# Mixed channels stored as a high and a low part, and a sample tile that carries both in one operand

## The chip, the cores and the metric

One core of a Trainium2 chip runs one program. Its engines are TensorE (PE, matrix products, and PEld for loading its stationary operand), VectorE (DVE), ScalarE (ACT), GpSimd (POOL) and SyncE (SP, which issues most transfers). Each engine takes its instructions in the order in which they stand. The metric is the device time of one execution in microseconds; lower is better.

## What is computed

One inference step of a layer for 1024 prompt tokens and 64 sample tokens, 1024 channels wide. A normalised input is projected once; its columns feed two head groups, and both are gated, joined to 2048 mixed channels and projected back:

```python
proj = h @ w_in
...
o = _diff_attend(q, k, v, ...)                    # group A: differential attention, 8 heads
y_a = o.reshape(bsz, t_len, A_WIDTH) * jax.nn.silu(proj[..., A_G:B_R].astype(F32))
...
yb, s_T = _wkv_scan(rh, hs(decay), kh, vh, -kk, kk * ah, wkv0.astype(F32))   # group B: RWKV-7
yb = (yb + bonus.reshape(bsz, t_len, B_WIDTH)) * jax.nn.silu(proj[..., B_G:IN_TOTAL].astype(F32))
mix = jnp.concatenate([y_a, yb], axis=-1).astype(x.dtype)
out = mix @ w_out
x_new = x + _rms_norm(out, norm_post, NORM_EPS)
```

## The kernel before

Products of float32 values are made from two parts: a high part (a cast to fp32r) and a low part (the rest). `split` (L155) makes them: ScalarE copies the value to the high part, GpSimd subtracts that from the value. A product of two such values is three matrix products: high by high, low by high, high by low.

The program is written by streams (Python generators) that `Weave` (L59) interleaves as it is built. A stream yields either a modelled time after which it may go on or a condition; the stream of lowest rank that can go on is taken next. `spend` adds to the modelled time of TensorE, `op` books an operation on another engine and returns when it should be done. So the order on each engine is fixed when the program is built, and a change of these numbers changes it.

Head group B comes first (`phase_b`, L290): 17 units, of channel pair p and half hf of the prompt, and one of all pairs for the sample. A unit ends with its gated result `yo` (L941 to L964), channels by 512 tokens, which SyncE stores to the DRAM tile `mixd["B", hf]` (L969). The input projections are the filler between the units. Then comes attention (`phase_a`, L1238): per head h and query tile qt the streams `score` and `qtile`; after the last query tile of a group of four (or the sample's), the gated result `y` (L1485) goes to `mixd["A", j]` (L1487).

The filler of that stage is the output projection (`out_projection`, L1096). It works through 63 jobs (g, tt): 7 groups of four channel blocks (groups 0 to 5 with one half of the output columns, the last with both) by 9 token tiles, 8 of 128 prompt tokens and the sample's, number 8. `load_wo` loads and splits the weights of a group. `load_mix` (L1148) loads the job's 4 x 128 channels by 128 tokens to `raw` (two buffers, tag mxr; for the sample, zeros fill the 64 empty columns, L1157) and splits them to `hi` and `lo` (three buffers each, tags mxh and mxl). The loader starts a job's load when the job three back has been issued. A job is 12 products of 128 x 512 per column half:

```python
mm(ps, hi[:, q, :], wh, start=(q == 0), stop=False)
mm(ps, lo[:, q, :], wh, start=False, stop=False)
mm(ps, hi[:, q, :], wl, start=False, stop=(q == len(ks) - 1))
```

Their sum is added to `part[tt]` (L1225, L1228). In the last group `half_done` (L1180) squares each half on ScalarE, and `finish` (L1189) normalises the row, adds x and stores it; for tiles 3 and 8 a quarter of the columns goes to ScalarE and GpSimd. PSUM has two buffers for these sums (`pjp`).

Of the kernel before, what the change touches and what calls it, by code (L numbers as in the profile page):

```python
# [11 lines left out]
F32 = mybir.dt.float32  # L12
# [9 lines left out]
P = 128  # L22
# [95 lines left out]
def layer(ctx: ExitStack, tc: tile.TileContext, I, O):  # L118
# [76 lines left out]
    mixd = {(a, j): tc.dram_tile([D, n], F32, name=f"mix{a}{j}")  # L195
# [94 lines left out]
def phase_b(tc, I, O, E):  # L290
# [8 lines left out]
    with ExitStack() as bs:  # L299
# [203 lines left out]
        def unit(n, p, hf):  # L503
# [437 lines left out]
            yo = t512("ysq", 1, nm=f"o{u}")  # L941
            for g in range(2):
# [23 lines left out]
            if smp:  # L966
                nc.sync.dma_start(out=mixd["B", 2].rearrange("(q c) t -> c q t", c=P), in_=c3(yo))
            else:
                nc.sync.dma_start(out=mixd["B", hf][p * P:(p + 1) * P, :], in_=yo)  # L969
# [126 lines left out]
def out_projection(tc, I, O, E):  # L1096
# [24 lines left out]
    jobs = [(g, tt) for g in range(7) for tt in ((4, 5, 6, 7, 0, 1, 2, 3, 8) if g == LAST else range(9))]  # L1121
# [26 lines left out]
    def load_mix(q):  # L1148
# [6 lines left out]
        raw = op.tile([P, 4, P], F32, tag="mxr", bufs=2, name=f"mxr{g}{tt}")[:, 0:m]  # L1155
        if n < P:
            nc.gpsimd.memset(raw, 0.0)  # L1157
        r0 = (ks[0] % 8) * P
        nc.sync.dma_start(out=raw[:, :, 0:n], in_=src[r0:r0 + m * P, o_ * P:o_ * P + n].rearrange(
            "(k c) t -> c k t", c=P))  # L1160
        yield W_DMA
        hi = op.tile([P, 4, P], F32R, tag="mxh", bufs=MB, name=f"mxh{g}{tt}")[:, 0:m]
        lo = op.tile([P, 4, P], F32R, tag="mxl", bufs=MB, name=f"mxl{g}{tt}")[:, 0:m]
        yield split_op(hi, lo, raw, m * P)
        mix[q] = hi, lo
# [14 lines left out]
    def half_done(tt, ch):  # L1180

        if ch == 0:
            x_ = op.tile([P, D], F32, tag="x", bufs=2, name=f"fx{tt}")
            nc.scalar.dma_start(out=x_[:P if tt < 8 else TS], in_=x_rows(tt))
            fin[tt] = x_, op.tile([P, 2], F32, tag="ms", bufs=2, name=f"fm{tt}")
        sq = op.tile([P, 512], BF16, tag="sq", name=f"fs{tt}{ch}")
        act(sq, part[tt][:, ch * 512:(ch + 1) * 512], AF.Square, accum_out=fin[tt][1][:, ch:ch + 1])

    def finish(tt):  # L1189
# [3 lines left out]

        vts(ms[:, 0:1], ms[:, 0:1], ms[:, 1:2], D * NORM_EPS, op0=ADD, op1=ADD)
        gtt(ms[:, 0:1], ms[:, 0:1], nh[:, 0:1], op=POW)
        m = 768 if tt in (3, 8) else D
        a, b = o_[:, 0:m], o_[:, m:]
        if m < D:
            act(b, b, AF.Copy, scale=ms[:, 0:1])
        stt(a, a, ms[:, 0:1], npb[:, 0:m], op0=MUL, op1=MUL)  # L1200
        vtt(a[:n], a[:n], x_[:n, 0:m], op=ADD)
        if m < D:
            gtt(b, b, npb[:, m:], op=MUL)
            gtt(b[:n], b[:n], x_[:n, m:], op=ADD)
# [353 lines left out]
```

## Time and profile before

| | us |
|---|---|
| median of 3 runs | 1828.87 (1828.2 to 1833.91) |
| profiled execution | 1827.69 |
| its span | 1825.9 |
| PE busy in the span | 1685.0 (92%) |
| DVE | 1248.1 (68%) |
| ACT | 846.3 (46%) |
| POOL | 721.5 (40%) |

A busy share is a mean over stages. Group B fills the time to about 1260 us, attention the time to about 1740, the rest of the output projection the time to 1815. Matrix products are pipelined: one may start before the row of the one before has ended, so the distance of starts, not the duration of a row, tells what one of them takes of TensorE. A wait is put down to what came last before the instruction could start.

### The profile page before, as it was taken

The numbers are of one execution on the slowest core, as the hardware profiler recorded it, in microseconds if no ns is written. First come the engines' busy times: TensorE is split into PE (matmuls) and PEld (weight loads), VectorE is DVE, ScalarE is ACT, GpSimd is POOL, SyncE is SP. The second block draws the span as 40 slices with busy tenths as digits, with TensorE's granted clock in tenths as the row PEclk, the third lists the DMA queues.
The fourth block names the chain that finished last, engine by engine and source line by source line (L and its number), as shares of the span: only waits on it lengthen the run. The fifth ranks groups of instructions, "written<-read, shape, count | busy, mean of one in ns | idle before, by whom it ended". The sixth has DMA issues, their size and how long they took to land.

```text
span 1825.9 us, 34303 instructions
## 1 busy us (share of the span) xinstructions
PE 1685.0 (92%) x12930; PEld 1505.6 (82%) x12930; DVE 1248.1 (68%) x2600; ACT 846.3 (46%) x2026; POOL 721.5 (40%) x905
## 2 busy tenths in 40 slices
PE   5999989999998989999999989989998899988997
PEld 4988978889878888898898878989887777777885
DVE  5577777786777877778778567654466566677736
ACT  5334443444434444444444333333455665766632
POOL 3432332332332232333333333111443758667563
PEclk9999999999999999999999989999999899999999
DMA  5110123121132111121111121336745555644345
GB/s 154 53 56 26 51 64 91 33 65 49 44 85 64 33 52 33 30 67 30 42 46 31 59 70 46 106 105 152 183 121 151 162 157 162 165 123 123 96 137 165
DMA packets 204096, 158.82 MB, mean 87 GB/s; under 512 B 44085, under 2 KB 185050, under 8 KB 203930
## 3 DMA queue, kind: packets, MB, share of 16 engines
q1 hardware_dynamic: 169098, 137.33, 26.4%
q10 hardware_dynamic: 34832, 19.30, 4.1%
q8 instruction: 102, 1.67, 0.4%
q14 instruction: 64, 0.52, 0.1%
HBM read 108.67 MB, written 47.34 MB: 85 GB/s over the span
## 4 chain that ended last, share of the span: by engine, by line
PE 56%; DVE 19%; POOL 7%; DMA 6%; issue 5%; ACT 4%; ACTq 1%; SPq 1%; POOLq 0%; DVEq 0%
PE x_o L1456 2%; PE po L1217 2%; PE po L1218 2%; PE po L1219 2%; PE cbank L871 2%; PE cbank L843 2%; PE m_s L670 1%; PE pj_av L215 1%; PE s L1395 1%; PE cbank L860 1%; PE pj_av L216 1%; PE pj_av L217 1%; PE pj_g L215 1%; PE s L1396 1%; PE pj_aq L215 1%
## 5 line engine op out<-in xcount | busy, mean ns | idle before, releaser
L850 ACT ACTIVATE sd<-suv,dc 64x64 f32<-64x64 f32 x128 | 44.4, 347 | 178.3 <-DVE suv L881 151.1
L1217 PE MATMUL po<-woh,mxh 128*128 128x512 f32 x288 | 121.6, 422 | 1.5 <-DVE part L1228 0.9
L1219 PE MATMUL po<-wol,mxh 128*128 128x512 f32 x288 | 115.1, 400 | 1.8 <-POOL wol L158 1.8
L1218 PE MATMUL po<-woh,mxl 128*128 128x512 f32 x288 | 115.4, 401 | 0.9 <-POOL mxl L158 0.9
L1412 ACT ACTIVATE e<-s,nb 128x128 f32<-128x128 f32 (+7 forms) x144 | 101.1, 707 | 31.9 <-DVE nb L1405 20.8
L158 POOL TENSOR_TENSOR mxl<-mxr,mxh 128x512 fp32r<-128x512 f32 x63 | 88.2, 1401 | 54.9 <-ACT mxh L157 52.5
L1456 PE MATMUL x_o<-vn,wt 128*128 128x128 f32 (+1 forms) x608 | 87.1, 289 | 11.4 <-DVE wt L1446 3.7
L1456 PEld LDWEIGHTS x_o<-vn,wt 128*128 128x128 f32 (+1 forms) x608 | 80.0, 200 | 20.6 <-DVE wt L1446 5.2
L1405 DVE TENSOR_REDUCE nb<-s 128x1 f32<-128x640 f32 (+8 forms) x104 | 95.5, 921 | 2.0
L716 POOL TENSOR_TENSOR ltlo<-lt,lt 64x512 f16<-64x512 f32 x32 | 37.6, 1176 | 130.3 <-ACT lt L704 129.1
L1395 PE MATMUL s<-k,qs 128*128 128x512 f32 (+4 forms) x208 | 75.8, 372 | 7.8 <-ACT e L1412 6.0
L881 DVE SCALAR_TENSOR_TENSOR suv<-cbank,dc,sd 64x64 f32<-64x64 f32 x224 | 63.1, 282 | 29.2 <-PE cbank L871 24.2
L871 PE MATMUL cbank<-suv,bkt 128*128 128x128 f32 x256 | 56.4, 302 | 23.1 <-DVE suv L867 23.1
L215 PE MATMUL pj_k<-hhi,wh_k 128*128 128x384 f32 (+1 forms) x192 | 72.1, 375 | 3.8 <-ACT raw_k L230 3.8
L1396 PE MATMUL s<-k,qs 128*128 128x512 f32 (+4 forms) x208 | 70.6, 357 | 2.8 <-POOL k L1325 1.8
L215 PE MATMUL pj_av<-hhi,wh_av 128*128 128x384 f32 (+1 forms) x192 | 69.8, 363 | 2.3 <-DVE fl_g L980 2.1
L215 PE MATMUL pj_aq<-hhi,wh_aq 128*128 128x384 f32 (+1 forms) x192 | 70.8, 369 | 0.0
L215 PE MATMUL pj_g<-hhi,wh_g 128*128 128x384 f32 (+1 forms) x192 | 70.6, 368 | 0.0
L215 PE MATMUL pj_ak<-hhi,wh_ak 128*128 128x384 f32 (+1 forms) x192 | 70.2, 366 | 0.0
L871 PEld LDWEIGHTS cbank<-suv,bkt 128*128 128x128 f32 x256 | 41.3, 189 | 34.4 <-DVE suv L867 32.1
L215 PE MATMUL pj_v<-hhi,wh_v 128*128 128x384 f32 (+1 forms) x192 | 69.6, 363 | 0.0
L1228 DVE TENSOR_TENSOR part<-po,part 128x512 f32<-128x512 f32 x54 | 37.0, 686 | 47.0 <-PE po L1219 46.8
(525 smaller groups left out, 6044.1 us busy)
## 6 DMA issues: line engine op xcount, KB each, us to landing
mxr<-mixB SPq DMA_DIRECT2D x32, 256.0 KB
wor<-in_w_out SPq DMA_DIRECT2D x64, 128.0 KB
qa<-scr_q SPq DMA_DIRECT2D x32, 204.0 KB
ka<-scr_k SPq DMA_DIRECT2D x32, 204.0 KB
mxr<-mixA SPq DMA_DIRECT2D x24, 256.0 KB
scr_q<-fl_q SPq DMA_DIRECT2D x8, 544.0 KB
scr_k<-fl_k SPq DMA_DIRECT2D x8, 544.0 KB
scr_v<-fl_v SPq DMA_DIRECT2D x8, 544.0 KB
```

Of the source, the lines that this page charges most:

```text
L158: gtt(lo, raw, hi.bitcast(F32), op=SUB)
L215: mm(ps[:, :n], hi[:, k, :], hhi[i][:, k, :], start=(k == 0), stop=False)
L871: mm(s, bkt[:, c], suv[:, c], start=True, stop=True)
L881: stt(suv[r, c + 1, h, :] if c < 7 and not smp else to[r], s[r, h * CH:(h + 1) * CH], dc[r, c:c + 1], sd[r], op0=MUL, op1=ADD)
L1217: mm(ps, hi[:, q, :], wh, start=(q == 0), stop=False)
L1218: mm(ps, lo[:, q, :], wh, start=False, stop=False)
L1219: mm(ps, hi[:, q, :], wl, start=False, stop=(q == len(ks) - 1))
L1395: mm(s2[:, b:b + w], lq, k1[c][:, k0 + o_:k0 + o_ + w], start=True, stop=False)
L1396: mm(s2[:, b:b + w], lq, k2[c][:, k0 + o_:k0 + o_ + w], start=False, stop=True)
L1405: nc.vector.tensor_reduce(nb[:, 0:m], s3[:, :, 0:n], axis=AX.X, op=MAX, negate=True)
L1412: act(e[:, 0:n], s3[:, j, 0:n], AF.Exp, bias=nb[:, j:j + 1], accum_out=st["sm"][:, c:c + 1])
L1456: mm(ops[:, 0:P], wt[0:w, b, :], vn[0:w, vb, :], start=(b == 0), stop=(b == len(kbs) - 1))
```

## The change

Both parts of a mixed channel are made where it is made: at the end of a unit of group B (`yo` becomes the low part in place, `yh` the high part) and at the end of a group of query tiles in attention. Both are stored, in pieces of 128 tokens; the DRAM tile has the high and the low part of a token tile side by side. `load_mix` then loads both in one transfer of 512 KB (256 KB for the sample) straight into the products' operand `mx`, three buffers, with no split behind it and no zeros. For the sample, `mx` has 64 columns of high and 64 of low parts, so that one product yields high by weight in rows 0 to 63 and low by weight in rows 64 to 127: two products per block where there were three (low by low is added too). At the end the lower rows of `part[8]` are moved up by a transfer and added. In the last group the sample stands between tiles 7 and 0 and no longer at the end, and in attention its last head's sample tile between query tiles 4 and 3.

```diff
-    mixd = {(a, j): tc.dram_tile([D, n], F32, name=f"mix{a}{j}")
+    mixd = {(a, j): tc.dram_tile([D, n // min(n, P), 2, min(n, P)], F32, name=f"mix{a}{j}")
...
             yo = t512("ysq", 1, nm=f"o{u}")
+            yh = t512("yh", 1, F32R, nm=f"h{u}")
...
             op_(DVE, 512)
-            if smp:
-                nc.sync.dma_start(out=mixd["B", 2].rearrange("(q c) t -> c q t", c=P), in_=c3(yo))
-            else:
-                nc.sync.dma_start(out=mixd["B", hf][p * P:(p + 1) * P, :], in_=yo)
+            w = TS if smp else P
+            yl = yo.bitcast(F32R)
+            split(yh, yl, yo)
+            op_(ACT, 512)
+            yield op_(POOL, 512)
+            for s, t in ((0, yh), (1, yl)):
+                t_ = t.bitcast(F32).rearrange("p (c t) -> p c t", t=w)
+                if smp:
+                    nc.sync.dma_start(out=mixd["B", 2][:, 0, s].rearrange("(q c) t -> c q t", c=P), in_=t_)
+                else:
+                    nc.sync.dma_start(out=mixd["B", hf][p * P:(p + 1) * P, :, s], in_=t_)
             free.add(("g", p, hf))
...
-    jobs = [(g, tt) for g in range(7) for tt in ((4, 5, 6, 7, 0, 1, 2, 3, 8) if g == LAST else range(9))]
+    jobs = [(g, tt) for g in range(7) for tt in ((4, 5, 6, 7, 8, 0, 1, 2, 3) if g == LAST else range(9))]
...
-        raw = op.tile([P, 4, P], F32, tag="mxr", bufs=2, name=f"mxr{g}{tt}")[:, 0:m]
-        if n < P:
-            nc.gpsimd.memset(raw, 0.0)
         r0 = (ks[0] % 8) * P
-        nc.sync.dma_start(out=raw[:, :, 0:n], in_=src[r0:r0 + m * P, o_ * P:o_ * P + n].rearrange(
-            "(k c) t -> c k t", c=P))
+        mx = op.tile([P, 4, 2 * P], F32, tag="mx", bufs=MB, name=f"mx{g}{tt}")[:, 0:m, 0:2 * n]
+        nc.sync.dma_start(out=mx, in_=src[r0:r0 + m * P, o_].rearrange("(k c) s t -> c k (s t)", c=P))
         yield W_DMA
-        hi = op.tile([P, 4, P], F32R, tag="mxh", bufs=MB, name=f"mxh{g}{tt}")[:, 0:m]
-        lo = op.tile([P, 4, P], F32R, tag="mxl", bufs=MB, name=f"mxl{g}{tt}")[:, 0:m]
-        yield split_op(hi, lo, raw, m * P)
-        mix[q] = hi, lo
+        mix[q] = mx.bitcast(F32R)
...
     def half_done(tt, ch):
 
+        if tt == 8:
+
+            if ch == 0:
+                return
+            low = op.tile([P, D], F32, tag="x", bufs=2, name="low")[0:TS]
+            nc.sync.dma_start(out=low, in_=part[8][TS:P])
+            vtt(part[8][0:TS], part[8][0:TS], low, op=ADD)
+            half(tt, 0)
+        half(tt, ch)
...
-        m = 768 if tt in (3, 8) else D
+        m = 768 if tt in (2, 3) else D
...
-                mm(ps, hi[:, q, :], wh, start=(q == 0), stop=False)
-                mm(ps, lo[:, q, :], wh, start=False, stop=False)
-                mm(ps, hi[:, q, :], wl, start=False, stop=(q == len(ks) - 1))
-                spend(690)
+                end = q == len(ks) - 1
+                if tt == 8:
+
+                    mm(ps, mx[:, q, :], wh, start=(q == 0), stop=False)
+                    mm(ps, mx[:, q, :], wl, start=False, stop=end)
+                    spend(460)
+                else:
+                    mm(ps, mx[:, q, 0:P], wh, start=(q == 0), stop=False)
+                    mm(ps, mx[:, q, P:], wh, start=False, stop=False)
+                    mm(ps, mx[:, q, 0:P], wl, start=False, stop=end)
+                    spend(690)
...
-            xdone(op_(DVE, n_))
-            nc.sync.dma_start(out=mixd["A", j][h * P:(h + 1) * P, :], in_=y[:, 0:n_])
+            yield xdone(op_(DVE, n_))
+            yh = ap_.tile([P, HALF], F32R, tag="yh", name=f"yh{u}")
+            w = n_ // m
+            split(yh[:, 0:n_], y[:, 0:n_].bitcast(F32R), y[:, 0:n_])
+            op_(ACT, n_)
+            yield op_(POOL, n_)
+            for s, t in ((0, yh.bitcast(F32)), (1, y)):
+                nc.sync.dma_start(out=mixd["A", j][h * P:(h + 1) * P, :, s],
+                                  in_=t[:, 0:n_].rearrange("p (c t) -> p c t", t=w))
             yield 3000
...
-        for o_, qt in enumerate((0, 1, 8, 2, 3, 4, 5, 6, 7) if h < 7 else (7, 6, 5, 4, 3, 2, 1, 0, 8)):
+        for o_, qt in enumerate((0, 1, 8, 2, 3, 4, 5, 6, 7) if h < 7 else (7, 6, 5, 4, 8, 3, 2, 1, 0)):
```

GpSimd in group B, where the first unit (pair 0, first half) ends; `bk` belongs to the unit that follows it, `t_wus` is the split of a later unit's small weights, `wl_aq3` the low part of a projection weight. Before:

```order
L917 COPY ycp_517<-ycp_517 64x64
L634 TENSOR_TENSOR bk1_0_2371<-t_kb1_0_2026,t_cs1_0_1918 64x8x64
L425 MEMSET mv1_1_2447 128x64
L426 MEMSET mv1_1_2447 128x64
L533 TENSOR_TENSOR t_wus1_10_2609<-t_wup1_2477,t_wus1_10_2609 128x256
L158 TENSOR_TENSOR wl_aq3_2425<-wr_aq30_2426,wh_aq3_2424 128x512
L379 COPY sh_495<-raw_v1_2174 128x1
L380 COPY sh_495<-raw_v1_2174 128x1
```

Now:

```order
L918 COPY ycp_517<-ycp_517 64x64
L635 TENSOR_TENSOR bk1_0_2373<-t_kb1_0_2026,t_cs1_0_1918 64x8x64
L426 MEMSET mv1_1_2451 128x64
L427 MEMSET mv1_1_2451 128x64
L158 TENSOR_TENSOR ysq_o0_0_2298<-ysq_o0_0_2298,yh_h0_0_2299 128x512
L534 TENSOR_TENSOR t_wus1_10_2613<-t_wup1_2481,t_wus1_10_2613 128x256
L158 TENSOR_TENSOR wl_aq3_2429<-wr_aq30_2430,wh_aq3_2428 128x512
L380 COPY sh_495<-raw_v1_2174 128x1
```

The subtraction of `ysq_o0_0` by `yh_h0_0` stands ahead of the next unit's weight split.

SyncE where the output projection begins; `mxr00` and `mx00` are the first job's tile, `wor` pieces of w_out, `ka` the k rows of a later head. Before:

```order
L1357 DMA out_k_s<-kt82_17299 64x128
L1159 DMA mxr00_17230<-mixB0_123 128x4x128
L1141 DMA wor800_17234<-in_w_out 128x256
L1159 DMA mxr01_17236<-mixB0_123 128x4x128
L1301 DMA ga2_16804<-scr_g2_152 128x1088
L1141 DMA wor80256_17312<-in_w_out 128x256
L1360 DMA out_v_p<-vn2_16802 128x8x128
L1159 DMA mxr02_17291<-mixB0_123 128x4x128
L1361 DMA out_v_s<-vn2_16802 64x128
L1487 DMA mixA1_121<-y1_7_17349 128x512
L1141 DMA wor900_17354<-in_w_out 128x256
L1276 DMA ka30_17391<-rot_k02_166 16x1088
```

Now:

```order
L1380 DMA out_k_s<-kt82_17412 64x128
L1166 DMA mx00_17321<-mixB0_123 128x4x256
L1150 DMA wor800_17325<-in_w_out 128x256
L1166 DMA mx01_17327<-mixB0_123 128x4x256
L1166 DMA mx02_17331<-mixB0_123 128x4x256
L1150 DMA wor80256_17368<-in_w_out 128x256
L1150 DMA wor900_17397<-in_w_out 128x256
L1150 DMA wor90256_17407<-in_w_out 128x256
L1150 DMA wor1000_17430<-in_w_out 128x256
L1383 DMA out_v_p<-vn2_16878 128x8x128
L1384 DMA out_v_s<-vn2_16878 64x128
L1396 DMA out_k_p<-kt20_17439 128x8x64
```

Three tiles and five weight pieces stand ahead of the first `ka` transfer (it comes three rows later), where three tiles and three pieces stood.

VectorE in the last group: `po6` and then tile and column half are the sums, `fm` the statistics, `fx` the rows of x. Before, at the end:

```order
L1228 TENSOR_TENSOR part3_17221<-po631_21941,part3_17221 128x512
L1228 TENSOR_TENSOR part8_17226<-po680_21965,part8_17226 128x512
L1194 TENSOR_SCALAR fm3_21938<-fm3_21938 128x1
L1200 SCALAR_TENSOR_TENSOR part3_17221<-part3_17221,fm3_21938,npb_17227 128x768
L1201 TENSOR_TENSOR part3_17221<-part3_17221,fx3_21936 128x768
L1228 TENSOR_TENSOR part8_17226<-po681_21984,part8_17226 128x512
L1194 TENSOR_SCALAR fm8_21981<-fm8_21981 128x1
L1200 SCALAR_TENSOR_TENSOR part8_17226<-part8_17226,fm8_21981,npb_17227 128x768
L1201 TENSOR_TENSOR part8_17226<-part8_17226,fx8_21979 64x768
```

Now, where the sample is finished:

```order
L1251 TENSOR_TENSOR part8_17317<-po681_21689,part8_17317 128x512
L1251 TENSOR_TENSOR part0_17309<-po600_21716,part0_17309 128x512
L1251 TENSOR_TENSOR part0_17309<-po601_21735,part0_17309 128x512
L1191 TENSOR_TENSOR part8_17317<-part8_17317,low_21699 64x1024
L1251 TENSOR_TENSOR part1_17310<-po610_21758,part1_17310 128x512
L1210 TENSOR_SCALAR fm8_21704<-fm8_21704 64x1
L1216 SCALAR_TENSOR_TENSOR part8_17317<-part8_17317,fm8_21704,npb_17318 64x1024
L1210 TENSOR_SCALAR fm0_21732<-fm0_21732 128x1
L1217 TENSOR_TENSOR part8_17317<-part8_17317,fx8_21702 64x1024
L1216 SCALAR_TENSOR_TENSOR part0_17309<-part0_17309,fm0_21732,npb_17318 128x1024
L1251 TENSOR_TENSOR part1_17310<-po611_21777,part1_17310 128x512
L1217 TENSOR_TENSOR part0_17309<-part0_17309,fx0_21730 128x1024
```

The addition of `low` stands behind both sums of tile 0, and the sample's steps between those of tiles 0 and 1.

## Rows read from the trace of the kernel before

**Rows 1.** The head and PE's part of the page's first part

```profile
span 1825.9 us, 34303 instructions
PE 1685.0 (92%) x12930; PEld 1505.6 (82%) x12930; DVE 1248.1 (68%) x2600; ACT 846.3 (46%) x2026; POOL 721.5 (40%) x905
```

**Rows 2.** By stretch, us: length; PE, PEld, DVE, ACT, POOL busy; clock; DMA share

```profile
100.00:1300.00 1200.00, 1129.82 (x9766) 1032.70 (x9765) 860.77 (x1905) 493.75 (x1119) 369.25 (x434) 0.99 0.22 62
1400.00:1740.00 340.00, 308.11 (x1784) 255.72 (x1784) 225.63 (x431) 216.15 (x591) 224.25 (x286) 0.96 0.52 143
1740.00:1764.00 24.00, 23.67 (x104) 19.05 (x103) 5.84 (x9) 8.77 (x20) 20.80 (x24) 1.00 0.50 148
1764.00:1815.00 51.00, 50.15 (x220) 40.77 (x218) 33.00 (x41) 17.46 (x43) 16.36 (x18) 1.00 0.53 173
1815.00:1826.00 11.00, 0.25 (x2) 0.00 (x0) 4.68 (x6) 1.23 (x3) 4.91 (x5) 0.62 0.23 72
```

**Rows 3.** Timeline of PE; columns: start us, us, engine, line, operation

```profile
1740.32 0.39 PE L1218 MATMUL po<-woh,mxl 128*128 128x512 f32 x1
1740.55 0.39 PE L1219 MATMUL po<-wol,mxh 128*128 128x512 f32 x1
1740.77 0.39 PE L1217 MATMUL po<-woh,mxh 128*128 128x512 f32 x1
```

**Rows 4.** Instructions of the mix tile; ns are least, median, most

```profile
L157 ACT CAST mxh<-mxr x63: 603/620/667, 1413.6 to 1799.0; 128x512 fp32r<-128x512 f32 x63
L158 POOL TENSOR_TENSOR mxl<-mxr,mxh x63: 1263/1290/2447, 1414.3 to 1799.7; 128x512 fp32r<-128x512 f32 x63
L1157 POOL MEMSET mxr<- x7: 525/527/529, 1463.9 to 1790.4; 128x512 f32 x7
```

**Rows 5.** The gated result of attention (same view)

```profile
L1485 DVE SCALAR_TENSOR_TENSOR y<-x_z,dv,ga x24: 274/743/752, 1320.6 to 1736.2; 128x512 f32<-128x512 f32 x16, 128x64 f32<-128x64 f32 x8
```

**Rows 6.** Waits of PE from 1300 us; columns: total us, times, longest

```profile
PE s L1395 <- ACT e L1412: 6.0, 6, 2.5
```

**Rows 7.** Timeline of POOL and DVE in the last group

```profile
1784.65 1.29 POOL L158 TENSOR_TENSOR mxl<-mxr,mxh 128x512 fp32r<-128x512 f32 x1
1784.72 2.30 DVE L1200 SCALAR_TENSOR_TENSOR part<-part,fm,npb 128x1024 f32<-128x1024 f32 x1 [0.73 <-POOL fm L1195]
...
1792.29 1.28 DVE L1200 SCALAR_TENSOR_TENSOR part<-part,fm,npb 128x1024 f32<-128x1024 f32 x1 [0.67 <-POOL fm L1195]
```

**Rows 8.** Waits of SyncE's queue from 1300 us

```profile
SPq L1159 <- POOL mxl L158: 77.1, 35, 5.8
```

**Rows 9.** Issue and cast of a load (timeline); the chain's longest load

```profile
1758.68 3.10 SPq L1159 DMA_DIRECT2D mxr<-mixA  x2
1761.47 0.62 ACT L157 CAST mxh<-mxr 128x512 fp32r<-128x512 f32 x1 [1.45 <-DMA mxr<-mixA]
...
1409.24 6.83 DMA mxr<-mixB
```

**Rows 10.** Group B: a unit's last step, a weight split, a PE wait

```profile
L964 DVE TENSOR_TENSOR ysq_o<-ysq_o,mg x16: 680/687/693, 207.6 to 1261.8; 128x512 f32<-128x512 f32 x16
...
L158 POOL TENSOR_TENSOR wl_v<-wr_v,wh_v x16: 1266/1376/1836, 67.8 to 964.7; 128x512 fp32r<-128x512 f32 x16
...
PE cbank L871 <- DVE suv L867: 23.1, 23, 3.2
```

**Rows 11.** Instructions of the result rows on DVE

```profile
L1228 DVE TENSOR_TENSOR part<-po,part x54: 664/691/692, 1497.8 to 1816.5; 128x512 f32<-128x512 f32 x54
L1200 DVE SCALAR_TENSOR_TENSOR part<-part,fm,npb x9: 1017/1285/2301, 1772.9 to 1818.9; 128x1024 f32<-128x1024 f32 x7, 128x768 f32<-128x768 f32 x2
L1201 DVE TENSOR_TENSOR part<-part,fx x9: 1207/1225/1366, 1774.7 to 1819.9; 128x1024 f32<-128x1024 f32 x7, 128x768 f32<-128x768 f32 x1, 64x768 f32<-64x768 f32 x1
```

**Rows 12.** The last product (timeline); the queue's wait for the last store

```profile
1814.86 0.39 PE L1219 MATMUL po<-wol,mxh 128*128 128x512 f32 x1
...
SPq L1554 <- DMA out_xs<-part: 2.4, 1, 2.4
```

More of the change, by code (lines that the diff above doesn't have):

```diff
@@ L1180, in half_done, with half @@
     def half_done(tt, ch):
+        if tt == 8:
[6 more added lines that the diff above has]
+        half(tt, ch)
+    def half(tt, ch):
+        n = P if tt < 8 else TS
         if ch == 0:
             x_ = op.tile([P, D], F32, tag="x", bufs=2, name=f"fx{tt}")
-            nc.scalar.dma_start(out=x_[:P if tt < 8 else TS], in_=x_rows(tt))
+            nc.scalar.dma_start(out=x_[:n], in_=x_rows(tt))
             fin[tt] = x_, op.tile([P, 2], F32, tag="ms", bufs=2, name=f"fm{tt}")
         sq = op.tile([P, 512], BF16, tag="sq", name=f"fs{tt}{ch}")
-        act(sq, part[tt][:, ch * 512:(ch + 1) * 512], AF.Square, accum_out=fin[tt][1][:, ch:ch + 1])
+        act(sq[:n], part[tt][:n, ch * 512:(ch + 1) * 512], AF.Square, accum_out=fin[tt][1][:n, ch:ch + 1])
     def finish(tt):
@@ L1192, in finish @@
         x_, ms = fin.pop(tt)
+        ms = ms[:n]
         vts(ms[:, 0:1], ms[:, 0:1], ms[:, 1:2], D * NORM_EPS, op0=ADD, op1=ADD)
-        gtt(ms[:, 0:1], ms[:, 0:1], nh[:, 0:1], op=POW)
-        m = 768 if tt in (3, 8) else D
-        a, b = o_[:, 0:m], o_[:, m:]
+        gtt(ms[:, 0:1], ms[:, 0:1], nh[:n, 0:1], op=POW)
+        m = 768 if tt in (2, 3) else D
+        a, b = o_[:n, 0:m], o_[:n, m:]
         if m < D:
             act(b, b, AF.Copy, scale=ms[:, 0:1])
-        stt(a, a, ms[:, 0:1], npb[:, 0:m], op0=MUL, op1=MUL)
-        vtt(a[:n], a[:n], x_[:n, 0:m], op=ADD)
+        stt(a, a, ms[:, 0:1], npb[:n, 0:m], op0=MUL, op1=MUL)
+        vtt(a, a, x_[:n, 0:m], op=ADD)
         if m < D:
-            gtt(b, b, npb[:, m:], op=MUL)
-            gtt(b[:n], b[:n], x_[:n, m:], op=ADD)
+            gtt(b, b, npb[:n, m:], op=MUL)
+            gtt(b, b, x_[:n, m:], op=ADD)
         dst = O["xp"][0, tt * P:(tt + 1) * P, :] if tt < 8 else O["xs"][0]
@@ L1210, in out_projection @@
         yield lambda: g in ws and i in mix
-        hi, lo = mix.pop(i)
+        mx = mix.pop(i)
         ks, chs = groups[g]
@@ L1241, in phase_a @@
     nh, ident, hsl = (E[k] for k in ("nh", "ident", "hsl"))
-    scr, mixd, mixed, weave = (E[k] for k in ("scr", "mixd", "mixed", "weave"))
+    scr, mixd, mixed, weave, split = (E[k] for k in ("scr", "mixd", "mixed", "weave", "split"))
     projected, roped = E["projected"], E["roped"]
```

## Prediction

> **What bounds the kernel now.** I read the page's busy shares first, then the busy time by stage, then single starts on TensorE, then the waits. TensorE is busy for 1685.0 of 1825.9 us [rows 1]; no other engine is above 68%. By stages [rows 2] the reader is to see three different pictures. From 100 to 1300 us (head group B with projections woven in) TensorE is busy 1129.82 of 1200 us, so 70.2 us are idle. From 1400 to 1740 (attention with the output projection woven in) it is busy 308.11 of 340, 31.9 us idle. From 1740 to 1815 only the output projection is left: 23.67 of 24 and 50.15 of 51. There TensorE alone is the bound, and its products start 0.227 us apart (1740.32, 1740.55, 1740.77) though a row says 0.39, because they are pipelined [rows 3]. So in that stretch a product that goes is worth 0.227 us, not the 0.40 of a mean duration. The end is an in-order TensorE queue: its work plus its idle time, plus the last 11 us, in which it is busy for 0.25 [rows 2].
>
> **Products that go.** Each product in L1217 to L1219 is one of three per channel block and column half. The sample has 16 blocks and 2 halves, so with pairs in place of triples 32 of its 96 products go. 32 x 0.227 = 7.3 us. Sixteen of them (groups 4, 5 and the last) belong to the stretch in which nothing else runs before, 3.6 us; the other sixteen stand among attention work, where idle time could take their place. I take -7.3, bounds -3.6 and -7.3, since in an in-order queue the work behind them moves up.
>
> **Splits that go, in the attention stage.** Before, each of 63 jobs has a cast of 0.62 on ScalarE and a subtraction of 1.29 (median) on GpSimd, 7 also a memset of 0.53 [rows 4]: 39.1, over 81 and 3.7 us. 24 new splits come back, after each y; 16 are 512 columns wide [rows 5], at the same prices 10 and 21 us, 8 have 64 columns and cost less. GpSimd loses some 60 of the 224.25 us that it is busy from 1400 to 1740, ScalarE some 27 of 216.15 [rows 2]. Neither is the bound, so this is not a gain by itself; it is one only where TensorE waits for them or for VectorE. Such waits are there, each short: the longest in sum are scores waiting for the exponential on ScalarE, 6.0 us in 6 waits [rows 6]. VectorE gains too: at 1784.72 a product-and-scale took 2.30 us while GpSimd's subtraction (1784.65, 1.29 us) ran, the same step at 1792.29 beside no such work took 1.28, so 1.02 us of collision [rows 7]. The Trainium skill (SBUF — State Buffer, section "Who interferes with whom") says that a VectorE instruction with two SBUF inputs contends with a GpSimd instruction that reads SBUF, and the second blocks for the whole of the first; that would make it about 1.22 + 1.28 = 2.50 here, and the row's 2.30 is near it. Idle time of 31.9 us cannot shrink by more than half, since most of it waits for TensorE's own results to come round; bounds 0 and -16, and I take -4, nearer the waits that rows name than the whole.
>
> **A wait that is added.** The load of a tile now writes straight into the operand (3 buffers), so it waits on SyncE for the products of the job three back; before, it waited for GpSimd's subtraction, 77.1 us in 35 waits [rows 8]. Queued behind it on SyncE are the next head's q and k loads, weights and stores, as before. In the pure stretch two jobs lie between, 24 products or 5.45 us; while attention runs it is longer. A 256 KB load took 2.8 us (issued 1758.68, cast released at 1761.47) when little else moved and 6.83 at 1409.24 in a crowd [rows 9]. The new load is twice the bytes in as many pieces, and no row shows it. At 2.8 it costs nothing; at 6.83 it misses by 1.4 us per job, for the five or so narrow jobs left in that stretch: +7. In the last group the two jobs take 10.9 us and cover either. I take 0, bounds 0 and +7. SyncE's order at the start of the output projection now has three loads and five weight pieces ahead of the next head's k loads, where three loads and three pieces stood; the share of the transfer engines from 1400 to 1740 is 0.52 [rows 2], so there is room, and I count nothing.
>
> **Splits that come, in group B.** 17 units get a cast, a subtraction and a second store behind their last VectorE step. The step before them takes 0.69, and a subtraction of this size among projections 1.38 [rows 10]. No later step of the same unit waits for them; what is queued behind them on GpSimd is the next unit's weight split, as the order shows. With the cast and a collision on VectorE, a unit costs 0.62 + 1.38 + 1.02 = 3.0 us at most if all of it lands on TensorE's path, 51 in all; nothing if it falls into idle time (GpSimd is busy 369.25 of 1200 us). TensorE's largest named wait there is for VectorE's copies in the state chain, 23.1 us in 23 waits [rows 10], so a VectorE that is held up can reach TensorE. I take +3, near the lower end, bounds 0 and +51. The changed waits also reorder some projections; that has no sign.
>
> **The end of the last group.** The sample moves before tiles 0 to 3, and its low half comes by a transfer and an addition on VectorE. The order puts both adds of tile 0 ahead of that addition, so a transfer of 2.8 us is hidden by 5.45 us of products. VectorE's load is then two adds of 0.69, 1.28 and 1.23 per tile [rows 11], 3.9 of 5.45 us, and the sample's 1.2 more in one place: TensorE can be held for a buffer once, I reckon 1 us, and the collisions above that go were worth up to 0.85 us of idle. Net 0, bounds -0.9 and +3. The last store is of 128 rows, not 64: the queue waits 2.4 us for 256 KB now [rows 12], bounds 0 and +2.4, I take +0.5. The tail from the last product (1814.86, [rows 12]) keeps its steps.
>
> **Sum.** -7.3 - 4 + 0 + 3 + 0 + 0.5 = -7.8 us. The profiled execution has a span of 1825.9 in 1827.69 us, so 1819.9 for its like. The median of the runs is 1828.87, 1.2 above the profiled one; **1821**.
>
> **Rivals.** (a) The attention stage tightens to its bound, -16 in place of -4: 1809. For it: GpSimd stands between statistics and transposes all through that stage, and the collisions on VectorE go. Against it: TensorE names few waits for GpSimd. (b) The products go but idle time takes their place outside the pure stretch: -3.6, relief 0, +3, +0.5, so 1829, no change. For it: 31.9 us idle in short waits for results that are no faster. Against it: the filling work is never short there. (c) Slower: the new splits in group B sit ahead of the next unit's weight split on GpSimd and hold VectorE. Half of their full price, 26 in place of 3, gives +15: 1844. It decides from about 1 us per unit (16.3 us in all, against the 10.8 of the other terms, for 5.5 more than before). For it: VectorE's state chain is what TensorE waits for. Against it: the splits lie off every chain. If VectorE alone is held, 17 collisions of 1.02 us [rows 7] that all reach TensorE add 17 in place of 3: 1835, at the edge of slower. The Trainium skill's rule above is what would make VectorE block wherever the two overlap. That the sample keeps its triples is no rival: the change writes pairs.
>
> **How the numbers follow.** Forecast 0.55 (its own range 1813 to 1827), (a) 0.13, (b) 0.20, (c) 0.12, of which 0.04 for the collisions alone. A difference under 0.3%, 5.5 us, can hardly be told from none. Below 1823.4 lie (a) and 0.45 of the forecast: faster 0.58. Between lie 0.10 of the forecast and (b): same 0.30. Slower 0.12. The range reaches from (a) to past (b), 1808 to 1833, and leaves out (c) and little else.
>
> **What would show it.** Right: 32 products fewer in the output projection; TensorE's idle time in the attention stage some 4 us below 31.9; group B's end within a few us of where it was; no wait of TensorE for the tile's load above 1 us in all. Wrong: TensorE waiting for the load (the wait of three jobs), VectorE's busy time in group B up by more than 10 us (c), an idle stretch at the sample's addition, or an idle time between the two that has moved by more than the saving.

## Result: slower by 2.9%, lost in two places

The changed kernel takes 1884.16 us (median of 4 runs, 1878.64 to 1890.19) against 1828.53 us of the kernel before: a ratio of 1.029, 95% interval 1.027 to 1.032. The forecast was 1821 us, a gain; the range 1808 to 1833 did not hold the time. The profiled execution took 1885.55 us. Its page begins, as [rows 1] did for the kernel before:

```profile
span 1883.8 us, 34243 instructions
...
PE 1709.2 (91%) x12898; PEld 1521.4 (81%) x12898; DVE 1245.9 (66%) x2601; ACT 833.6 (44%) x2004; POOL 675.8 (36%) x876
```

GpSimd has lost 45.7 us of work and ScalarE 12.7, as foreseen, and the span is longer by 58. So the work that went was not on the path. The question is by stage: I cut both executions at the same events, the last transposes of group B's last unit (1256.6 before, 1284.0 after), the first tile load of the output projection (1408, 1437.5), the last store of attention's results (1736.5, 1816) and the last product. Busy times by stretch: columns are length, then PE, PEld, DVE, ACT, POOL busy, then the granted clock, the share of the transfer engines and GB/s. The kernel before:

```profile
100.00:1256.60 1156.60, 1090.46 (x9548) 995.78 (x9546) 843.00 (x1868) 476.81 (x1082) 358.21 (x425) 0.99 0.20 57
1256.60:1408.00 151.40, 141.26 (x894) 129.53 (x892) 85.52 (x175) 81.53 (x213) 58.22 (x78) 0.97 0.59 150
1408.00:1736.50 328.50, 298.38 (x1728) 247.59 (x1727) 221.18 (x418) 209.47 (x568) 217.73 (x279) 0.96 0.52 144
1736.50:1815.00 78.50, 77.32 (x338) 62.73 (x336) 39.94 (x52) 28.43 (x68) 39.52 (x44) 1.00 0.51 162
```

and the changed kernel:

```profile
100.00:1284.00 1184.00, 1100.09 (x9543) 1005.41 (x9541) 850.35 (x1870) 486.78 (x1101) 376.01 (x443) 0.98 0.21 59
1284.00:1437.50 153.50, 144.76 (x916) 133.73 (x914) 89.11 (x177) 84.03 (x219) 65.52 (x85) 0.96 0.58 154
1437.50:1816.00 378.50, 330.43 (x1781) 266.17 (x1780) 215.93 (x423) 199.85 (x556) 181.96 (x263) 0.91 0.62 176
1816.00:1875.00 59.00, 56.04 (x244) 45.18 (x242) 35.45 (x47) 12.82 (x35) 7.67 (x10) 1.00 0.68 216
```

Group B is 27.4 us longer with the same products. The output projection, from its first load to its last product, is 29.9 us longer (437.1 against 407.2) with 32 products fewer: attention's part has grown by 50 us, and more of the projection was done in it, so the rest is 19.5 shorter. In attention's part TensorE idles 48.1 us where it idled 30.1, and the granted clock is 0.91 where it was 0.96. If TensorE were never idle, that would be (1 - 0.91) x 378.5 = 34 us against 13, an estimate from above.

### The profile page after: what moved, and what is told of

Same layout as the page of the kernel before. It is cut to its first block, busy times and chain, and to the rows that moved or that the text cites. A ratio compares the mean times of both kernels' runs of the same rounds, so it can differ in the third digit from the quotient of the medians.

```text
span 1883.8 us, 34243 instructions
## 1 busy us (share of the span) xinstructions
PE 1709.2 (91%) x12898; PEld 1521.4 (81%) x12898; DVE 1245.9 (66%) x2601; ACT 833.6 (44%) x2004; POOL 675.8 (36%) x876
## 3 DMA queue, kind: packets, MB, share of 16 engines
q1 hardware_dynamic: 200554, 162.10, 29.9%
## 4 chain that ended last, share of the span: by engine, by line
PE 42%; DVE 16%; POOL 6%; issue 4%; ACT 3%; DMA 3%; ACTq 0%; POOLq 0%; SPq 0%; DVEq 0%
PE x_o L1479 3%; PE po L1242 2%; PE po L1240 2%; PE po L1241 2%; PE s L1418 2%; PE s L1419 2%; PE pj_ag L216 1%; PE x_wt L1465 1%; PE cbank L872 1%; PE pj_ag L217 1%; PE pj_ag L218 1%; PE m_s L671 1%; POOL wol L158 1%; DVE xt L738 1%; PE cbank L861 1%
## 5 line engine op out<-in xcount | busy, mean ns | idle before, releaser
L1435 ACT ACTIVATE e<-s,nb 128x256 f32<-128x256 f32 (+8 forms) x144 | 100.7, 706 | 51.9 <-DVE nb L1428 37.0
L1240 PE MATMUL po<-woh,mx 128*128 128x512 f32 x256 | 111.9, 437 | 6.1 <-ACT woh L157 3.0
L1242 PE MATMUL po<-wol,mx 128*128 128x512 f32 x256 | 105.9, 415 | 11.6 <-POOL wol L158 11.5
L1241 PE MATMUL po<-woh,mx 128*128 128x512 f32 x256 | 105.4, 412 | 0.0
L872 PE MATMUL cbank<-suv,bkt 128*128 128x128 f32 x256 | 56.8, 304 | 20.9 <-DVE suv L868 20.9
L1469 DVE COPY wt<-x_wt 128x512 f32<-128x512 f32 (+3 forms) x64 | 37.1, 586 | 57.3 <-PE x_wt L1465 57.0
L1242 PEld LDWEIGHTS po<-wol,mx 128*128 128x128 f32 x256 | 50.3, 197 | 27.1 <-POOL wol L158 16.9
```

What stands on the lines that cost most here:

```text
L872: mm(s, bkt[:, c], suv[:, c], start=True, stop=True)
L1240: mm(ps, mx[:, q, 0:P], wh, start=(q == 0), stop=False)
L1241: mm(ps, mx[:, q, P:], wh, start=False, stop=False)
L1242: mm(ps, mx[:, q, 0:P], wl, start=False, stop=end)
L1435: act(e[:, 0:n], s3[:, j, 0:n], AF.Exp, bias=nb[:, j:j + 1], accum_out=st["sm"][:, c:c + 1])
```

## Experiments on group B: the plan or the work

The theories: the split's own work slows the units, or the bookings and the pause behind it have moved the projections in the plan. Four kernels tell them apart. The first two start from the changed kernel.

```diff
 # b_nobook
             split(yh, yl, yo)
-            op_(ACT, 512)
-            yield op_(POOL, 512)
 # b_nosplit
-            split(yh, yl, yo)
...
-            for s, t in ((0, yh), (1, yl)):
+            for s, t in ((0, yl), (1, yl)):
```

> The changed kernel, but the plan no longer counts the group-B split: its two bookings and the pause behind it are left out, the split and its two stores are still issued. TensorE's order up to the last unit of group B is then that of the kernel before, row for row; with the bookings 1608 of its 11256 rows stand elsewhere. The last unit's transposes of the changed kernel end 27 us later than before (1284 against 1257). Theory order (the moved projections cost it): they end within 6 us of 1257 and the kernel takes about 1857. Theory split work (cast, subtraction and the second store cost it, 1.3 us in each of units 2 and 3, which stand before any row is moved): they end at 1279 to 1284 and the kernel takes 1879 to 1884.

> The changed kernel with the plan's bookings kept, but group B's cast and subtraction left out: the whole value is stored into both slots (so the B part of the result counts the value twice). TensorE's order is that of the changed kernel; stores, bytes and loads are the same. Theory order: nothing comes back, the last unit's transposes end at about 1284 and the kernel takes about 1884. Theory split work: they end at 1257 to 1263 and the kernel takes about 1860.

b_nobook: 1860.06 us, the last unit's transposes at 1266. b_nosplit: 1869.15 us, 1275. Both theories hold in part: of group B's 27 us some 18 are order and some 9 are work (1266.2 - 1256.6 = 9.6 with the old order and the splits; 1284.0 - 1275.3 = 8.7 when the splits go). The order's part was then put on the kernel before by itself:

```diff
 # before_book
             op_(DVE, 512)
+            op_(ACT, 512)
+            yield op_(POOL, 512)
```

> The kernel before, with the two bookings and the pause that the change has behind group B's last step, and nothing else: no instruction is added or left out, the plan alone reckons with a split that does not exist. Earlier runs put 18 of the 27 us that group B got longer down to the moved projections (the changed kernel without the bookings ended its last unit's transposes at 1266, with them at 1284). Theory order: here they end at 1272 to 1278 in place of 1257, and the kernel takes 1842 to 1852. Theory that the order costs only beside real splits: 1257 to 1262, and 1829 to 1835.

1850.20 us, ratio 1.012 (1.009 to 1.016), the transposes at 1277.7: 21 us for two numbers and a pause, with no work added on any engine. TensorE's waits in group B (to 1290 us in the changed kernel, to 1256 in the others) are its signature. Columns: who waited for whom, us in total, times, longest. Before, b_nobook, before_book, changed kernel:

```profile
PE m_ip L723 <- DVE x L742: 7.3, 8, 2.5
...
PE cbank L860 <- DVE gsb L857: 4.6, 8, 1.8
```

```profile
PE m_ip L724 <- DVE x L743: 7.3, 8, 2.5
...
PE cbank L861 <- DVE gsb L858: 6.7, 9, 1.8
```

```profile
PE m_ip L723 <- DVE x L742: 18.7, 14, 2.7
...
PE cbank L860 <- DVE gsb L857: 14.0, 15, 2.3
```

```profile
PE m_ip L724 <- DVE x L743: 18.7, 14, 2.7
...
PE cbank L861 <- DVE gsb L858: 15.9, 17, 2.3
```

The pairs go with the order, not with the splits. The longest wait of [rows 10], for suv, does not go with them (23.1, 27.5, 18.0 and 20.9 us), so the pairs are no full account: in all, TensorE idles 66, 72, 78 and 84 us in group B. A unit's inverse (m_ip) and state chain (cbank) wait for VectorE's answer, and the projections that had stood in these gaps stand elsewhere. What moved them is one statement: the unit marks its gate tile free behind the pause, so the plan's next choice of a projection is r of pair 3 where it was g of pair 2, and everything behind shifts.

```diff
 # freeg
             split(yh, yl, yo)
+            free.add(("g", p, hf))
             op_(ACT, 512)
             yield op_(POOL, 512)
...
-            free.add(("g", p, hf))
```

> The changed kernel with one statement moved: group B's unit marks its gate tile as free right behind the last step that reads it, ahead of the bookings and the pause for the split, where the change marks it behind the pause. Bookings, pause, instructions and loads stay. The next gate projection may then be taken up as early as in the kernel before, and TensorE's order up to the last unit of group B is that of the kernel before, row for row. Theory late mark (what group B lost to its order hangs on this one mark): the last unit's transposes end at 1264 to 1270 in place of 1284, and the kernel takes 1856 to 1866. Theory that the bookings hurt in another way: 1278 to 1284 and 1878 to 1886.

1859.04 us, transposes at 1266.8, as without the bookings: the late mark is the whole cost of the order in group B.

The single differences hold to a few us only, as the kernels further down show, each of which has one of the two orders in group B row for row. The last transposes stand at 1279.6 to 1288.8 in seven kernels with the new order and the splits, at 1266.2 to 1270.5 in five with the old order and the splits, at 1275.3 and 1277.7 with the new order and no split, and at 1255.6 to 1262.5 in four with neither. By their medians the order costs 17 to 20 us and the splits 8 to 10.

## Experiments on the output projection

The changed kernel's longest waits from 1437 to 1816 us, of TensorE and of SyncE's queue; then the kernel before, its waits for the weights from 1408 to 1737 us:

```profile
PE po L1242 <- POOL wol L158: 11.5, 8, 3.3
PE s L1418 <- ACT e L1435: 9.4, 9, 4.2
...
SPq L1166 <- PE po L1242: 67.2, 27, 13.2
SPq L1150 <- POOL wol L158: 59.1, 25, 19.9
```

```profile
PE po L1219 <- POOL wol L158: 1.8, 2, 1.5
...
SPq L1141 <- POOL wol L158: 13.1, 12, 4.5
```

TensorE waits for the low parts of the weights, each time among the first 20 products of a group (groups 0, 2, 3 and 4); the tile loads, which I had worried about, cost it one wait of 0.5 us. SyncE stands still for TensorE (a tile's buffer, L1166) and for GpSimd (a weight's buffer, L1150). The first two theories, buffers and pacing:

```diff
 # mx5: and the x tiles of the end come from the same ring
-        mx = op.tile([P, 4, 2 * P], F32, tag="mx", bufs=MB, ...)
+        mx = op.tile([P, 4, 2 * P], F32, tag="mx", bufs=MB + 2, ...)
 # pace: in the changed kernel
         yield W_DMA
+        op_(ACT, m * P)
+        yield op_(POOL, m * P)
         mix[q] = mx.bitcast(F32R)
 # before_nopace: in the kernel before
-        yield split_op(hi, lo, raw, m * P)
+        split(hi, lo, raw)
```

> The changed kernel with five buffers in place of three for the tiles of the output projection (the buffers of x for the end stand in the same ring, so the memory is the same); the plan and TensorE's order up to group B's end are the same. A tile's load then never waits on SyncE for the products of the job three back (67 us in 27 waits in the attention stage of the changed kernel). Theory load behind products (SyncE stands still there, and the weights and the next head's loads behind it come late): the stretch from the first load to the last store of attention falls from 378 us towards the 329 of the kernel before, and the kernel takes 1850 to 1865. Theory pacing (the products come in bursts because the plan no longer waits for a split, whatever the buffers): 1880 to 1886.

> The changed kernel, but the plan still books a cast and a subtraction for each tile of the output projection, as before, though none is issued: a tile counts as ready later, and its jobs are spread as in the kernel before. Three buffers as in the changed kernel. Theory pacing: the attention stretch falls from 378 us towards 329, and the kernel takes 1850 to 1865. Theory load behind products: the load still waits for the job three back, the stretch stays above 365 us and the kernel takes 1872 to 1886.

> The kernel before, with the loader's cast and subtraction issued as ever but not booked in the plan, so that a tile counts as ready when its load does; no instruction is added or left out. Theory pacing (jobs in bursts hold up attention, whatever is loaded): the time from the first tile load to the last product of the output projection grows from 407 us by 12 to 25 and the kernel takes 1840 to 1855. Theory load or split work: 1826 to 1834.

mx5: 1877.69 us, and the wait is still there, only for an older job, since SyncE runs ahead as far as it is let (1395 to 1830 us, where the changed kernel has 77.4 in 31 waits):

```profile
SPq L1166 <- PE po L1242: 73.5, 22, 21.0
```

So it did not take away what it was meant to. pace: 1871.93 us; attention's part falls to 343 us, but fewer products are done in it and the rest grows to 77, so from first load to last product it is 420 us. before_nopace: 1828.26 us, ratio 1.000 (0.998 to 1.002), though 602 products were done by attention's end in place of 528. Pacing alone costs the kernel before nothing: that theory fell. pace's 12 us then hang on something else that the change brought; that it is the doubled loads, which pace spreads, is argued and not shown. The next two put the old order and the old bytes to it:

```diff
 # asbefore: no bookings for the new splits, those of load_mix kept, old places of the sample
 # halfload
+        if tt == 8: ...  # as in the changed kernel
-        nc.sync.dma_start(out=mx, in_=src[r0:r0 + m * P, o_]...)
+        nc.sync.dma_start(out=mx[:, :, 0:n], in_=src[r0:r0 + m * P, o_, 0]...)
...
-                    mm(ps, mx[:, q, P:], wh, start=False, stop=False)
+                    mm(ps, mx[:, q, 0:P], wh, start=False, stop=False)
```

> All of the changed kernel's instructions in nearly the old order: no bookings for the splits in group B and in attention, bookings kept for a split per tile though none is issued there, and the old places of the sample in the last group and in head 7. Theory plan (order and pacing are what was lost, apart from some 9 us for the splits in group B, less 7 for the products): 1828 to 1838. Theory transfers (the doubled loads, waiting for the job three back): the output projection still takes 15 to 25 us more than the 407 us before, and the kernel takes 1845 to 1860.

> The changed kernel in its own order, with tiles 0 to 7 loading only the high part (256 KB in place of 512), from which all three products of a block then read; the low part's contribution is thus wrong, and the products and their times are the same. Theory bytes (the doubled loads come late and crowd the other transfers): the attention stretch falls from 378 us to 350 to 362 and the kernel takes 1855 to 1870. Theory plan (order and pacing): 372 to 380 us, and 1878 to 1886.

asbefore: 1853.15 us, 416 us for the output projection. That lies between the theories: with the old plan 21 of the 30 us are gone, and 9 stay, below the 15 to 25 of the theory of transfers. Its time lies in that theory's range with the help of the end: the sample stands last again, with its transfer and addition behind it, and 19.3 us pass from the last product to the end of the span, 11.0 in the kernel before. halfload: 1847.60 us, attention's part 345 us: 37 us hang on the second half of each load, more than the theory of bytes had expected. Together with the old order in group B:

> The changed kernel without group B's bookings (the old order in group B) and with tiles 0 to 7 loading the high part alone (256 KB, the products as many, the low part's contribution thus wrong). Each of the two gave something back by itself, 24 and 37 us. If order and bytes are separate costs, this takes 1820 to 1828: what is left against the kernel before is then the splits in group B (some 9 us) less the 32 products (7). If they share a cost, 1832 to 1848.

1827.33 us, ratio 0.999 (0.997 to 1.001). The two causes add up: 57 us in place of 24 + 37. SyncE still waits as long in halfload (80.6 us in 32 waits at L1169, its tile load, from 1395 to 1830 us), so a wait of that queue is not a cost by itself. What matters is what stands behind it. Three kernels move one stream of transfers to ScalarE's queue:

```diff
 # mx5q (in mx5) and q3 (in the changed kernel)
-        nc.sync.dma_start(out=mx, ...)
+        nc.scalar.dma_start(out=mx, ...)
 # wq (in the changed kernel)
-                nc.sync.dma_start(out=raw, in_=I["w_out"]...)
+                nc.scalar.dma_start(out=raw, in_=I["w_out"]...)
 # before_q (in the kernel before)
-        nc.sync.dma_start(out=raw[:, :, 0:n], ...)
+        nc.scalar.dma_start(out=raw[:, :, 0:n], ...)
```

> The changed kernel with five tile buffers as in the run before that had them, and the tile loads issued from ScalarE's queue in place of SyncE's, so that weights and the next head's loads no longer stand in one queue behind 512 KB of tile. Bytes as in the changed kernel; some rows of attention and output projection change places. Theory queue (the doubled load costs because the smaller loads wait behind it in the same queue): the attention stretch falls from 374 us to 345 to 355 and the kernel takes 1845 to 1860. Theory bandwidth (the transfers share the same engines wherever they are issued): 365 to 378 us, and 1870 to 1884.

> The changed kernel with its three tile buffers, and the tile loads issued from ScalarE's queue. Five buffers alone gave back 6 us, five buffers and the other queue 51. Theory queue alone: 1830 to 1845. Theory both needed: a load that waits for the products of the job three back now holds up ScalarE's own work (exponentials, casts) behind it, and the kernel takes 1860 to 1884.

> The changed kernel with three buffers and its 512 KB tile loads on SyncE's queue, but the 64 weight pieces of the output projection (128 KB each) issued from ScalarE's queue. Moving the tile loads gave back 48 us. TensorE's longest named wait in the attention stretch of the changed kernel is for the last step of such a piece (11.5 us in 8 waits). Theory weights (the pieces come late because they stand behind the tile loads): most of it comes back here too, 1835 to 1850. Theory rest of the queue (the next head's loads and the stores behind the tile loads cost, not the weights): 1865 to 1886.

> The kernel before with its 256 KB tile loads issued from ScalarE's queue in place of SyncE's, the rest as ever. Theory that the one queue was a cost already before the change: the attention stretch falls from 329 us to 305 to 318, and the kernel takes 1805 to 1820. Theory that it became one through the doubled load and its wait: 1824 to 1834.

mx5q: 1832.75 us. q3: 1835.65 us, so 48 of the 51 us need no more buffers. wq: 1841.98 us: with the tile loads left where they were and only the weights moved, 42 come back. before_q: 1844.68 us, 0.7% slower (0.4 to 1.0%), outside the ranges of both theories. The kernel before gains nothing by the move, so the gain hangs on what the change brought. That the move also has a cost of its own, which hides a gain here, is not excluded. In wq the waits of TensorE for the weights are gone, while SyncE waits for TensorE as long as before (PE waits from 1432 to 1771 us, SP waits from 1437 to 1816; stretch of attention):

```profile
PE po L1240 <- ACT woh L157: 0.8, 1, 0.8
PE po L1242 <- POOL wol L158: 0.4, 1, 0.4
...
SPq L1166 <- PE po L1242: 70.8, 27, 5.6
...
1432.60:1770.70 338.10, 307.58 (x1779) 252.56 (x1778) 217.85 (x423) 198.27 (x556) 185.92 (x263) 0.96 0.69 197
```

How the streams hold each other up is seen in SyncE's own rows of the changed kernel (start, us, line, transfer):

```profile
1466.03 0.38 SPq L1516 DMA_DIRECT2D mixA<-y  x1
1466.46 21.49 SPq L1150 DMA_DIRECT2D wor<-in_w_out  x3
1488.88 1.28 SPq L1166 DMA_DIRECT2D mx<-mixB  x2
```

Three weight pieces took 21.49 us to issue, 19.9 of them waiting for a raw buffer that GpSimd was to free; the tiles of jobs 3 and 4 came behind them, at 1488.88. Meanwhile the transfer engines had next to nothing to do (share 0.07), so this delay is no lack of bandwidth:

```profile
1467.00:1487.90 20.90, 16.41 (x83) 12.73 (x81) 14.96 (x20) 13.84 (x32) 13.30 (x15) 0.84 0.07 18
```

How much such a delay costs TensorE, its named waits do not tell: those for the weights sum to 14.5 of the 48.1 us that it idles in attention's part.

A reservation: the builder itself moves rows when a load gets shorter or changes queues. In halfload, wq, mx5q and q3 between 672 and 894 of this stage's TensorE rows (some 2630) stand elsewhere than in the changed kernel, 127 to 370 of them by more than 12 places. No run here holds the order fixed and changes the transfers alone. Against order as the cause: seven kernels of different orders with the doubled tile loads and the weights both on SyncE take from first load to last product 416 to 445 us (changed kernel 437, b_nobook 426, b_nosplit 432, freeg 445, mx5 431, pace 420, asbefore 416), and six without that, of different orders too, 383 to 406 (halfload 403, nobook_half 406, mx5q 383, q3 390, wq 397 and the last one below 394). freeg and that last one reach their first load with fewer products done, so the count from group B's last transposes to the last product is fairer: 566 to 590 us against 535 to 557, and 558 in the kernel before. before_q takes 420 from its first load without any doubled load, so the move is not free either. How much of it is the held-up issue and how much the longer transfer, they do not separate.

## The pairs alone, and the change without its two costs

```diff
 # pair24, in the kernel before: the tile of the sample
+            yield split_op(hi[:, :, 0:n], hi[:, :, n:2 * n], raw[:, :, 0:n], m * P)
...
+                elif g < LAST:
+                    mm(ps, hi[:, q, :], wh, start=(q == 0), stop=False)
+                    mm(ps, hi[:, q, :], wl, start=False, stop=end)
```

> The kernel before, loads and splits as ever, with one part of the change alone: where the tile of the sample is split, its 64 high and 64 low columns go into one operand, and groups 0 to 5 take two products for it in place of three; the last group keeps three, and the low half is moved and added while it runs. The plan's prices stay, so the order stays. 24 products fewer at 0.227 us are 5.4 us, and 7 memsets go. Theory products count in full: 1821 to 1825, ratio 0.997. Theory idle time takes their place (16 of the 24 stand among attention work): 1826 to 1830.

1828.82 us, ratio 0.999 (0.998 to 1.001), at most some 4 us of gain. From first load to last product it takes 406.4 us, as before (407.0): TensorE is busy some 5 us less and idles as much more. In the kernel before, the products that go count for little or nothing.

> The changed kernel with both causes taken away: the gate tile marked free ahead of the pause (group B in the old order), and the tile loads on ScalarE's queue with five buffers. Each gave something back by itself, 25 us and 51 us. Theory separate causes: 1884 - 25 - 51 = 1808, so 1804 to 1816, below the kernel before. Theory shared cost (the attention stage cannot go lower, or its place in time matters): 1820 to 1833.

1810.91 us, ratio 0.988 (0.986 to 0.991): faster than both kernels. Its stretches, cut at the same events:

```profile
100.00:1266.70 1166.70, 1095.45 (x9546) 1001.53 (x9545) 850.71 (x1870) 485.87 (x1099) 382.89 (x441) 0.98 0.21 60
1266.70:1409.00 142.30, 131.50 (x831) 122.69 (x830) 82.59 (x161) 77.24 (x197) 54.94 (x75) 0.96 0.61 159
1409.00:1737.50 328.50, 308.12 (x1821) 258.07 (x1820) 221.32 (x434) 203.79 (x576) 186.91 (x271) 0.96 0.76 202
1737.50:1803.00 65.50, 63.74 (x276) 51.70 (x274) 36.69 (x50) 13.54 (x37) 8.56 (x12) 0.99 0.67 212
```

Group B is 10 us longer than before (the splits), the stretch behind it 9 shorter, with 63 products fewer in it, and the output projection takes 394 us in place of 407 at 202 GB/s: attention's part is as long as before, idles 20.4 us in place of 30.1, and gets more of the projection done.

## Why the prediction was wrong, point by point

- **A wait that is added (0, bounds 0 to +7): the step that failed first.** I asked whether a tile lands in time for its own products. It does: 0.5 us. I then wrote that behind it on SyncE stand the next head's loads, weights and stores "as before", and that with a transfer share of 0.52 "there is room, and I count nothing". The room was there (freeg_mx5q runs at 0.76), but one in-order queue could not use it. Measured: 37 us by half the bytes, 42 by moving the weights, 48 by moving the tiles. The plan has a part in it: spread out as before, the doubled loads leave the output projection at 420 (pace) or 416 us (asbefore) in place of 437, while the kernel before loses nothing without that spreading (before_nopace).
- **"The changed waits also reorder some projections; that has no sign": the step that failed second.** It has: +17 to +21 us, by a mark set late. The order listing of the two kernels would have shown the first swapped projection; I looked at what the change adds to a queue, not at what the plan then chooses.
- **Splits in group B (+3, bounds 0 to +51): mis-sized.** They cost 8 to 10 us, 0.5 to 0.6 per unit. Rival (c) had their work decide; its sign came true with a third of its term, and the order did the rest. The row of the changed kernel shows a price as assumed (1.38), and VectorE's busy time in group B grew by 7.4 us, below the 10 that I had named as the sign of (c):

```profile
L158 POOL TENSOR_TENSOR ysq_o<-ysq_o,yh_h x16: 1277/1340/1680, 210.4 to 1288.2; 128x512 fp32r<-128x512 f32 x16
```

- **Products (-7.3) and relief of attention (-4).** The 32 products are gone (832 in place of 864 in the output projection). Alone, 24 of them bring -1 (interval -4 to +2) where -5.4 was expected: rival (b), idle time in their place, was right for the kernel before. No relief is seen in the changed kernel: TensorE idles 18 us more in attention's part. The relief was also read too large, for the 60 us of GpSimd's work count all 63 jobs, of which 44 stood in that stage; it loses 36 there (217.73 to 181.96). With both costs away (freeg_mx5q) the output projection is 13 us shorter and the stretch ahead of it 9, more than 7.3 + 4. But that kernel also has two more buffers and its tile loads on another queue, so it does not measure these two terms, and no run does so in the changed kernel.
- **The end (0, and +0.5).** From the last store of attention on, TensorE idles 3.0 of 59 us (1.2 of 78.5 before), and the last product starts at 1874.20, 9.6 before the span's end, where it was 11.0 [rows 12]. Right.
- **Signs named.** "TensorE's idle time in the attention stage some 4 us below 31.9" and "group B's end within a few us" came out false, "no wait of TensorE for the tile's load above 1 us in all" came out true and was the wrong thing to watch: the queue's other customers show a queue's cost.

## What to carry to other kernels

When a transfer in an in-order queue grows or gets a new wait, list every stream that stands behind it and look for the one whose consumer has the least slack; here that was the weights, not the transfer's own reader. Where a planner sets the order, a delay in front of a flag is a change of order: compare the two orders row by row and take the first row that differs as a term of the sum. And a share of 0.5 on the transfer engines says nothing of how long one queue's head waits.

## What the runs showed of the hardware

In two places of the changed kernel the granted clock fell behind a stretch in which TensorE had idled in pieces, and that made the loss larger. Windows of the changed kernel, and its products beside them (0.42 us apart at 0.50, that is 1.2 GHz, and 0.23 at 1.00, 2.4 GHz):

```profile
1432.00:1442.80 10.80, 6.89 (x47) 5.30 (x47) 7.50 (x20) 5.31 (x20) 2.77 (x5) 1.00 0.59 174
1442.80:1463.30 20.50, 14.99 (x50) 11.61 (x51) 9.58 (x23) 8.40 (x29) 9.04 (x16) 0.50 0.89 273
1463.30:1480.30 17.00, 13.58 (x82) 10.26 (x80) 14.18 (x23) 12.92 (x30) 7.00 (x11) 1.00 0.28 81
1532.00:1538.30 6.30, 3.58 (x22) 2.52 (x20) 5.79 (x10) 5.59 (x11) 2.65 (x3) 1.00 0.22 60
1538.30:1548.50 10.20, 6.54 (x17) 4.74 (x18) 6.72 (x6) 3.22 (x7) 6.42 (x7) 0.50 0.30 74
...
1453.56 0.63 PE L1241 MATMUL po<-woh,mx 128*128 128x512 f32 x1
1453.98 0.63 PE L1242 MATMUL po<-wol,mx 128*128 128x512 f32 x1
...
1472.77 0.40 PE L1418 MATMUL s<-k,qs 128*128 128x512 f32 x1
1473.00 0.40 PE L1419 MATMUL s<-k,qs 128*128 128x512 f32 x1
```

TensorE was busy for 6.89 of the 10.8 us ahead, at full clock, and then ran at half for 20.5 us; later it was busy for 3.58 of 6.3 us and then ran at half for 10.2. That the idle time brought the fall is the reading that fits; no run tests it. What the clock costs is best read from wq, which has as many products in attention's part (1779 rows against 1781) at 0.96 in place of 0.91: TensorE is busy for 307.58 us in place of 330.43 and idles 30.5 in place of 48.1. Of the 40 us between the two some 23 go with the clock and 18 are idle time.

Moving one stream of transfers from SyncE's to ScalarE's queue gave 42 and 48 us of 1884 in one kernel and cost 15 of 1829 in the other. The Trainium skill (DMA: Bandwidth & Descriptors, section "Issuing engines are not separate DMA queues") says that transfers started by several engines run on the same transfer engines and that spreading them saves only the time to initiate them. By that rule moving the tile loads would have saved SyncE the time of 63 issues and TensorE nothing, in either kernel. Here the measurement decides, and it differs both ways. That it turns on which engine's waits stand in front of which stream is the reading that fits, though the order on TensorE moved too.
